# Gates of dense blocks scattered into cleared DRAM matrices by GpSimd, instead of built by one-hot products on TensorE

## The chip, the cores and the metric

The kernel runs on one core of a Trainium2 chip. The metric is the device time of one execution in microseconds; the kernel before took 3555.77 us (median of 3 runs, 3546.34 to 3557.35).

## What is computed

The reference is one decoder layer over 1024 tokens of width 1024: two mixers (sliding-window attention and a chunked mLSTM) make `x`, and then a PEER layer (an expert layer with 16384 experts of one hidden unit each) is added. The change touches the PEER layer alone:

```python
q = (xb @ w_query).reshape(t, PEER_HEADS, 2, PEER_KEY_DIM // 2)
s = jnp.einsum('thpd,hpkd->thpk', q, sub_keys)
top_s, top_i = lax.top_k(s, K)                     # K = 16 of 128, for both halves
cand_s = (top_s[:, :, 0, :, None] + top_s[:, :, 1, None, :]).reshape(t, PEER_HEADS, K * K)
cand_i = (top_i[:, :, 0, :, None] * N_KEYS + top_i[:, :, 1, None, :]).reshape(t, PEER_HEADS, K * K)
best_s, best_pos = lax.top_k(cand_s, K)
idx = jnp.take_along_axis(cand_i, best_pos, axis=-1)
gate = jax.nn.softmax(best_s, axis=-1)
act = jax.nn.gelu(jnp.einsum('td,thkd->thk', xb, expert_down[idx]), approximate=False)
out = jnp.einsum('thk,thkd->td', gate * act, expert_up[idx])
```

Each token picks 16 experts in each of 8 heads, 128 in all; two heads of a token may pick the same expert, and then their gates add up.

## The kernel before

The 1024 tokens are 8 blocks of 128, one token per partition, worked on in four groups of two blocks, (0,1) to (6,7). `front` runs the mixers of a group on TensorE: it ends with the output projection, whose four additions into `x` are L614 (called the x2 adds here), the PEER query and the scores, which go to DRAM (`sc_d`). `topk` then finds the experts of a block on VectorE. It is emitted by `later` with a low priority, so that the scheduler puts the top-k of one group between the rows of the next group's front. The weight strips of a front are split into a high and a low part, the low part on VectorE (L215, 50 such splits to a group), and TensorE waits for both.

PEER is worked out in two ways. Blocks 0, 6 and 7 (`SPARSE`) fetch the rows of their 128 experts by indirect DMAs from GpSimd (`fetch`, L743): per slot `down` gathers a row for every token and VectorE multiplies and sums it (L756), and `up` gathers another and VectorE adds it (L770). `down` of block 0 is run inside the fronts, its 128 sums spread over them by order edges (`pace`), with its gathers in a ring of two buffers. Blocks 1 to 5 (`DENSE`) go through all 16384 experts by matrix products (`dense`, in 32 steps of four rows of 128 experts): `hidden` makes the activations of all 640 tokens (L809), L816 multiplies them with a gate that is zero where a token did not pick the expert, and `outputs` adds the products with the up rows (L830 to L834).

That dense gate matrix is what the change is about. Before, `spread` makes it: the two parts of an expert's number and the gates are transposed, and for each token VectorE builds two one-hot matrices of 128x128 (L727 and L730; ScalarE makes one in four, L732 and L733), whose product over the token's 128 slots on TensorE (L735) is the token's 128x128 gate matrix; repeated experts add up in it. ScalarE copies four tokens to `stage` (L736), and 16 tokens go to `gate_d` by one DMA (L738), 64 numbers to a run. `fill` puts these quads between the rows of the last projections of the next group, three to every four pieces of a projection. A step of `dense` reads its 1280 KB of `gate_d` in one DMA (L841).

Each engine takes its instructions in the order in which the scheduler has put them into the program; the SP and GpSimd queues are in order too. DMAs from GpSimd signal through eight semaphores in turn (DMASW0 to 7), so the ninth waits for the first to land.

Of the kernel before, what the change touches and what calls it, by code (L numbers as in the profile page):

```python
# [10 lines left out]

F32 = mybir.dt.float32
# [5 lines left out]
AX = mybir.AxisListType  # L18
PSUM = bass.MemoryType.PSUM
NOSYNC = mybir.DependencyInfo(mybir.DependencyClass.NoSync, mybir.DependencyReason.DATA)  # L20

P = 128
S = 1024
# [11 lines left out]
SPARSE = (0, 6, 7)  # L35
DENSE = (1, 2, 3, 4, 5)
ND = P * len(DENSE)
GT = 16
GJ = 4
EG = 4  # L40
LATER = 5000
QUADS = 0.75
PACE0, PACE1 = 0.4, 0.95
WB = 4
PD0, PD1 = 0.06, 0.98
# [9 lines left out]
def layout(inputs):  # L55
# [5 lines left out]
    a = {}  # L61
# [21 lines left out]
    a["tri"] = tri  # L83
    a["freq"] = (500000.0 ** (-np.arange(0, 16, 2) / 16.0)).astype(np.float32)[None]
    a["iota"] = np.arange(P, dtype=np.float32)[None]
    return {k: np.ascontiguousarray(v) for k, v in a.items()}


def build(nc, tc, a, out, dbg=None):
# [4 lines left out]
    bp = pool("blocks", 2, outer)  # L94
    dp = pool("dram", 1, outer, space=bass.MemoryType.DRAM)
    kp = pool("topk", 2)
    ks = pool("spread", 1)
    gp = pool("gather", 2)
    st = pool("state", 1)
    wp = pool("weights", 1)  # L100
    fp = pool("front", 1)
# [8 lines left out]
    def const(name, shape, src=None, dt=F32, pool=None):  # L110
        t = (pool or cp).tile(shape, dt, name=name)
        SY.dma_start(t, a[name] if src is None else src)
        return t

    def probe(name, ap, idx=None):
        if dbg is not None and name in dbg:
            SY.dma_start(dbg[name] if idx is None else dbg[name][idx], ap)

    def bcast(name, n, pool=None):
        return const(name, [P, n], a[name].to_broadcast([P, n]), pool=pool)  # L120
# [10 lines left out]
    gains = const("gains", [P, 3, NC], pool=st)  # L131
    x_first = []
    pos = const("pos", [P, NB], dt=I32, pool=st)
    freq = bcast("freq", 8, st)
    qkg = bcast("qkg", 128, st)
    wifr = t4([P, NC, 16], "wifr")
# [54 lines left out]
    xb_d = dp.tile([NB, P, D], F32, name="xb_d")  # L191
    xbT_d = dp.tile([len(DENSE), P, NC, P], F32, name="xbT_d")
    sc_d = dp.tile([NB, 2, P, 8, P], F32, name="sc_d")
    gate_d = dp.tile([P, P // GJ, ND // GT, GJ, GT], F32, name="gate_d")

    RING = 3
    kT = st.tile([P, 2, RING, P], F32, name="kT")
# [9 lines left out]
    def wpart(i, q, split):  # L207
        t = wp.tile([P, 4, 256], F32, name="w", bufs=WB)
        SY.dma_start(t, a["wmain"][i, :, 4 * q:4 * q + 4, :])
        if not split:  # L210
            return t, None
        hi = wp.tile([P, 4, 256], F32R, name="whi", bufs=3)
        lo = wp.tile([P, 4, 256], F32R, name="wlo", bufs=3)
        A.copy(hi, t)  # L214
        V.tensor_tensor(lo, t, hi.bitcast(F32), ALU.subtract)  # L215
        return hi, lo
# [430 lines left out]
    def topk(b):  # L647
# [15 lines left out]
        for qh in range(4):  # L663
# [23 lines left out]
            for p, n in ((0, 17), (1, 16)):  # L687
# [4 lines left out]
                V.tensor_tensor(eqh, eqh, tif[:, :, p, None, 0:n].to_broadcast([P, 2, 16, n]), ALU.mult)  # L692
                V.tensor_reduce(ef[:, p, cols], eq, AX.X, ALU.add)
        gate = (bp.tile([P, 8, 16], F32, name="gate", bufs=len(SPARSE)) if b in SPARSE
                else ks.tile([P, 8, 16], F32, name="dgate", bufs=2))
        V.tensor_tensor(gate, bv, bv[:, :, 0:1].to_broadcast([P, 8, 16]), ALU.subtract)
        A.activation(gate, gate, AF.Exp)
        gs = kp.tile([P, 8], F32, name="gsum")
# [1 line left out]
        V.reciprocal(gs, gs)  # L700
        V.tensor_tensor(gate, gate, gs[:, :, None].to_broadcast([P, 8, 16]), ALU.mult)
        r = {"gate": gate}
        if b in SPARSE or dbg:
            r["idx"] = idx = bp.tile([P, P], I32, name="idx", bufs=len(SPARSE))
            V.scalar_tensor_tensor(idx, ef[:, 1], 128.0, ef[:, 0], ALU.mult, ALU.add)
            probe("idx", idx, b)
            probe("gate", gate, b)
        if b in DENSE:
            r["spread"] = spread(ef, gate, DENSE.index(b))
        return r  # L710

    def spread(ef, gate, k):
        cols = ks.tile([P, 3, P], F32, name="cols")
        ps = ptp.tile([P, 4, P], F32, name="tp")
        for n, src in enumerate((ef[:, 0], ef[:, 1], gate.rearrange("p h k -> p (h k)"))):
            T.transpose(ps[:, n, :], src, ident)
        A.copy(cols, ps[:, 0:3, :])
        for c in range(P // GT):
            stage = ks.tile([P, P, GT], F32, name="stage", bufs=2)
            for q in range(GT // 4):  # L720
                ps = pat.tile([P, 4, P], F32, name="at")
                for u in range(2):
                    oi = ks.tile([P, 2, P], F32, name="oi", bufs=3)
                    oj = ks.tile([P, 2, P], F32, name="oj", bufs=3)
                    t = c * GT + 4 * q + 2 * u
                    for n in range(2):
                        V.tensor_scalar(oi[:, n], iota, cols[:, 0, t + n:t + n + 1], cols[:, 2, t + n:t + n + 1],  # L727
                                        ALU.is_equal, ALU.mult)
                        if n or u:
                            V.tensor_scalar(oj[:, n], iota, cols[:, 1, t + n:t + n + 1], None, ALU.is_equal)  # L730
                        else:
                            A.activation(oj[:, n], iota, AF.Square, scale=-1.0, bias=cols[:, 1, t + n:t + n + 1])  # L732
                            A.activation(oj[:, n], oj[:, n], AF.Relu, scale=-1.0, bias=1.0)  # L733
                    for n in range(2):
                        T.matmul(ps[:, 2 * u + n, :], oi[:, n], oj[:, n], start=True, stop=True)  # L735
                A.copy(stage[:, :, 4 * q:4 * q + 4], ps.rearrange("p t j -> p j t"))  # L736
                if q == GT // 4 - 1:
                    SY.dma_start(gate_d[:, :, k * (P // GT) + c], stage.rearrange("p (n g) t -> p n g t", g=GJ))  # L738
                yield

    def fetch(p, table, idx, s):
        t = p.tile([P, D], F32, name="g")
# [31 lines left out]
    def dense():  # L774
# [26 lines left out]
        def hidden(j, g):  # L801
# [10 lines left out]
                    mark("dense", ins)  # L812
            act = tp.tile([P, ND], F32, name="act", bufs=1)
            A.activation(act.rearrange("p (u t) -> p u t", u=NH), ps[:, :, 0:W], AF.Gelu)
            av_ = act.rearrange("p (c t) -> p c t", t=GT)
            V.tensor_tensor(av_, av_, g, ALU.mult)  # L816
            ah = tp.tile([P, ND], F32R, name="ah", bufs=EG + 1)
            al = tp.tile([P, ND], F32R, name="al", bufs=EG + 1)
            A.copy(ah, act)
# [17 lines left out]

        work = []
        for n in range(P // EG):
            g = tp.tile([P, ND // GT, GJ, GT], F32, name="g")  # L840
            SY.dma_start(g, gate_d[:, n])  # L841
            new = []
            for e in range(EG):
                new.append(hidden(EG * n + e, g[:, :, e, :]))
                if n == 0 and e == 0:
                    for k in range(nk):
                        SY.dma_start(y[:, k, :], x2_d[DENSE[k]])
                if e == 0 and work:
                    outputs(work, new[0][3].ins.name)
            work = new  # L850
# [5 lines left out]
    def later(blocks):  # L856
        now = tc.cur_priority
        tc.cur_priority = now + LATER
        for b in blocks:
            res[b] = topk(b)  # L860
        tc.cur_priority = now
        return [q for b in blocks if "spread" in res[b] for q in [res[b]["spread"]]]

    res = {}
    hT = normed(GROUPS[0])
    for n, g in enumerate(GROUPS):
        spreads = chain.from_iterable(later(GROUPS[n - 1])) if n else iter(())

        due = [0.0]

        def fill():
            due[0] += QUADS
            while due[0] >= 1.0:
                next(spreads, None)
                due[0] -= 1.0

        hT = front(g, fill, hT, GROUPS[n + 1] if n + 1 < len(GROUPS) else None)
        for _ in spreads:
            pass
    later(GROUPS[-1])  # L880
    names = anchors["front"]
    names = names[int(PACE0 * len(names)):int(PACE1 * len(names))]
# [24 lines left out]
```

## Time and profile before

| | |
|---|---|
| median of 3 runs | 3555.77 us |
| the profiled execution | 3545.12 us, its span 3543.4 us |
| TensorE (PE) | 3378.6 us busy, 95% of the span |
| VectorE (DVE) | 2743.1 us, 77% |
| ScalarE (ACT) | 1363.0 us, 38% |
| GpSimd (POOL) | 985.7 us, 28% |
| TensorE's mean granted clock | 0.966 of full speed |

The profile is of one execution on the chip. Busy time is the time in which an engine runs an instruction; what an engine waited for is inferred from semaphores. The fronts of the four groups take the first half of the span, to about 1748 us, and the dense stage the rest.

### The profile page before, as it was taken

Reading aid. Unit: us, or ns where it says so; the run is one execution under the profiler, and the core shown is the slowest. Engines: PE = TensorE matmul, PEld = TensorE weight load, DVE = VectorE, ACT = ScalarE, POOL = GpSimd, SP = SyncE. Lnnn points to the kernel's source line nnn. Section 1 sums busy time; section 2 is a strip of 40 time slices with the busy share of each in tenths; the row PEclk is TensorE's granted clock in tenths of the full one; section 3 lists DMA queues with packets and bytes.
Section 4 is the critical chain, followed back from the end, with each engine's and each line's share of the span. In section 5 each row is a group of like instructions: output and inputs, shape, how many; then the busy total and the mean of one; then the engine's idle time right before and its main releaser. Section 6 shows DMA issues by size and latency. Waiting matters only on the chain.

```text
span 3543.4 us, 55473 instructions
## 1 busy us (share of the span) xinstructions
PE 3378.6 (95%) x20579; PEld 3044.3 (86%) x20579; DVE 2743.1 (77%) x6406; ACT 1363.0 (38%) x2730; POOL 985.7 (28%) x772
## 2 busy tenths in 40 slices
PE   7999999999998789989799999999999999999999
PEld 7898988888887678887688898999989999898998
DVE  5332689739898468988598988888888888889985
ACT  6652567338574346635322222222222222222221
POOL 0000000110001221110004654545455455545542
PEclk9999999999999888999899999999999999999999
DMA  4344434874378874686727988889888888888884
GB/s 149 108 143 166 164 115 145 256 261 141 117 212 252 274 247 150 206 244 174 252 101 276 329 307 321 321 284 329 285 315 305 294 321 299 312 308 302 325 288 160
DMA packets 386670, 846.66 MB, mean 239 GB/s; under 512 B 189280, under 2 KB 195168, under 8 KB 382304
## 3 DMA queue, kind: packets, MB, share of 16 engines
q1 hardware_dynamic: 275808, 440.42, 37.7%
q0 software_dynamic: 110592, 402.70, 32.5%
q8 instruction: 162, 2.65, 0.3%
q14 instruction: 108, 0.88, 0.1%
HBM read 780.11 MB, written 62.91 MB: 238 GB/s over the span
## 4 chain that ended last, share of the span: by engine, by line
PE 66%; DVE 13%; issue 8%; DMA 7%; POOL 3%; ACT 3%; SPq 0%; POOLq 0%; DVEq 0%; ACTq 0%
PE ph L809 19%; PE pj L229 8%; PE po L830 6%; PE po L833 6%; PE po L834 6%; PE pj L231 4%; PE pj L233 4%; PE pj L232 4%; DMA g<-down,idx 3%; POOL g L743 3%; DVE oi L727 2%; PE at L735 2%; DMA w<-wmain 1%; DVE g L756 1%; DMA g<-up,idx 1%
## 5 line engine op out<-in xcount | busy, mean ns | idle before, releaser
L743 POOL DMA_INDIRECT g<-down,idx x384 | 480.2, 1250 | 1769.3 <-DVE act L756 879.2
L743 POOL DMA_INDIRECT g<-up,idx x384 | 505.3, 1316 | 732.8 <-DVE acc L770 373.9
L756 DVE CUSTOM_DVE_ANT_0 g<-g,xb 128x1024 f32<-128x1024 f32 x384 | 462.6, 1219 | 167.2 <-DMA g<-down,idx 166.6
L770 DVE SCALAR_TENSOR_TENSOR acc<-g,coef,acc 128x1024 f32<-128x1024 f32 x384 | 491.7, 1281 | 46.8 <-DMA g<-up,idx 36.8
L830 PE MATMUL po<-hu,ah 128*128 128x512 f32 x1280 | 499.2, 390 | 2.3 <-DVE y L836 2.3
L809 PE MATMUL ph<-xbh,hd 128*128 128x320 f32 x2048 | 470.6, 311 | 31.7 <-ACT hd L797 22.8
L833 PE MATMUL po<-lu,ah 128*128 128x512 f32 x1280 | 498.5, 389 | 0.0
L834 PE MATMUL po<-hu,al 128*128 128x512 f32 x1280 | 498.1, 389 | 0.0
L809 PE MATMUL ph<-xbh,ld 128*128 128x320 f32 x2048 | 470.5, 311 | 5.3 <-DVE ld L798 5.3
L809 PE MATMUL ph<-xbl,hd 128*128 128x320 f32 x2048 | 469.9, 311 | 0.0
L797 ACT CAST hu<-rawu 128x1024 fp32r<-128x1024 f32 x128 | 131.5, 1051 | 738.9 <-PE po L834 557.0
L809 PEld LDWEIGHTS ph<-xbh,hd 128*128 128x128 f32 x2048 | 346.6, 189 | 35.3 <-ACT hd L797 23.2
L215 DVE TENSOR_TENSOR wlo<-w,whi 128x1024 fp32r<-128x1024 f32 x200 | 243.3, 1218 | 142.1 <-ACT whi L214 142.0
L809 PEld LDWEIGHTS ph<-xbh,ld 128*128 128x128 f32 x2048 | 345.1, 189 | 7.0 <-DVE ld L798 6.7
L809 PEld LDWEIGHTS ph<-xbl,hd 128*128 128x128 f32 x2048 | 345.6, 189 | 0.0
L214 ACT CAST whi<-w 128x1024 fp32r<-128x1024 f32 x200 | 209.3, 1047 | 235.9 <-DMA w<-wmain 100.1
L836 DVE TENSOR_TENSOR y<-po,y 128x512 f32<-128x512 f32 x320 | 218.2, 685 | 89.0 <-PE po L834 88.5
L830 PEld LDWEIGHTS po<-hu,ah 128*128 128x128 f32 x1280 | 240.3, 188 | 53.9 <-DVE y L836 4.7
L834 PEld LDWEIGHTS po<-hu,al 128*128 128x128 f32 x1280 | 240.3, 188 | 50.5 <-DVE al L820 0.3
L833 PEld LDWEIGHTS po<-lu,ah 128*128 128x128 f32 x1280 | 240.3, 188 | 48.5
L232 PE MATMUL pj<-wlo,hT 128*128 128x256 f32 x832 | 244.9, 295 | 23.9 <-DVE wlo L215 23.9
L231 PE MATMUL pj<-whi,hT 128*128 128x256 f32 x832 | 245.9, 296 | 1.1 <-ACT whi L214 1.1
(266 smaller groups left out, 6670.2 us busy)
## 6 DMA issues: line engine op xcount, KB each, us to landing
w<-wmain SPq DMA_DIRECT2D x328, 512.0 KB
rawd<-downT SPq DMA_DIRECT2D x128, 512.0 KB
rawu<-up SPq DMA_DIRECT2D x128, 512.0 KB
gate_d<-stage SPq DMA_DIRECT2D x40, 1024.0 KB
g<-gate_d SPq DMA_DIRECT2D x32, 1280.0 KB
x<-x SPq DMA_DIRECT2D x16, 512.0 KB
sc_d<-sc SPq DMA_DIRECT2D x16, 512.0 KB
sc<-sc_d SPq DMA_DIRECT2D x32, 256.0 KB
```

Source lines behind the costliest of these rows:

```text
L215: V.tensor_tensor(lo, t, hi.bitcast(F32), ALU.subtract)
L229: ins = T.matmul(ps, lh(c), rh(c), start=first, stop=last)
L231: T.matmul(ps, lh(c), rh(c), start=first, stop=False)
L232: T.matmul(ps, lh(c), rl(c), start=False, stop=False)
L743: G.indirect_dma_start(out=t, out_offset=None, in_=a[table], in_offset=bass.IndirectOffsetOnAxis(ap=idx[:, s:s + 1], axis=0))
L756: ins = V.tensor_tensor_reduce(out=t, in0=t, in1=xb, scale=1.0, scalar=0.0, op0=ALU.mult, op1=ALU.add, accum_out=act[:, s:s + 1])
L770: ins = V.scalar_tensor_tensor(acc, t, g, acc, ALU.mult, ALU.add)
L809: ins = T.matmul(ps[:, u, 0:W], w[:, c, :], x[:, c, u * W:u * W + W], start=first, stop=last)
L830: first = T.matmul(o, ah[:, tok], uh[:, cols], start=(e == 0), stop=False)
L833: T.matmul(o, ah[:, tok], ul[:, cols], start=False, stop=False)
L834: ins = T.matmul(o, al[:, tok], uh[:, cols], start=False, stop=(e == EG - 1))
L836: V.tensor_tensor(y[:, k, cols], o, y[:, k, cols], ALU.add)
```

## The change

`spread`, `fill` and `QUADS` go. For each dense block there is now a matrix `gate_d[k]` in DRAM, indexed by expert row, expert column and token (128x128x128, 8 MB). `clear_part` writes zeros to all five in 160 DMAs of 256 KB from SP, one behind each of the first 160 weight DMAs. `topk` of a dense block also makes `cell`, the address of each of its gates, and `scatter` then issues 128 indirect DMAs from GpSimd (L734 of the changed kernel), each of which adds the gates of one slot, 128 numbers of 4 bytes, into `gate_d[k]`. Within a head the experts of a token differ, so its 16 DMAs may run together; the first DMA of a head has to wait for all 16 of the head before, since two heads may add to the same cell. A step of `dense` reads its gates by five DMAs of 256 KB instead of one of 1280 KB, in runs of 512 bytes. The ring of `down`'s gathers in the fronts has four buffers instead of two.

```diff
+    tokc = const("tokc", [P, 1], pool=st)
@@
-    gate_d = dp.tile([P, P // GJ, ND // GT, GJ, GT], F32, name="gate_d")
+    gate_d = [dp.tile([P, P, P], F32, name=f"gate_d{b}") for b in DENSE]
+    none = st.tile([P, P * P // ZP], F32, name="none")
+    V.memset(none, 0.0)
+    clear = iter([(k, z) for k in range(len(DENSE)) for z in range(ZP)])
+
+    def clear_part():
+        for k, z in [next(clear, (None, 0))]:
+            if k is not None:
+                SY.dma_start(gate_d[k].rearrange("j i t -> (j i t)").rearrange("(z p f) -> z p f", z=ZP, p=P)[z], none)
@@ def wpart
         SY.dma_start(t, a["wmain"][i, :, 4 * q:4 * q + 4, :])
+        clear_part()
@@ def topk
         if b in DENSE:
-            r["spread"] = spread(ef, gate, DENSE.index(b))
+            cell = ks.tile([P, P], I32, name="cell")
+            V.tensor_scalar(cell, idx, 128.0, tokc, ALU.mult, ALU.add)
+            r["cell"] = cell
@@
-    def spread(ef, gate, k):
...
+    def scatter(rs):
+        views = [bass_types.dram_disjoint_views(gate_d[k].rearrange("j i t -> (j i t)")[:, None], 16) for k, _ in rs]
+        done = [[] for _ in rs]
+        for h in range(8):
+            for n, (k, r) in enumerate(rs):
+                new = []
+                for s in range(16):
+                    c = 16 * h + s
+                    ins = G.indirect_dma_start(
+                        out=views[n][s], out_offset=bass.IndirectOffsetOnAxis(ap=r["cell"][:, c:c + 1], axis=0),
+                        in_=r["gate"].rearrange("p h k -> p (h k)")[:, c:c + 1], in_offset=None, compute_op=ALU.add)
+                    if s == 0:
+                        for d in done[n]:
+                            tc.add_manual_dep(ins.ins, d, SYNC, reason="heads")
+                    else:
+                        after(ins, new[0])
+                    new.append(ins.ins.name)
+                done[n] = new
@@ def dense
-            g = tp.tile([P, ND // GT, GJ, GT], F32, name="g")
-            SY.dma_start(g, gate_d[:, n])
+            g = tp.tile([P, nk, EG, P], F32, name="g")
+            for k in range(nk):
+                SY.dma_start(g[:, k], gate_d[k][EG * n:EG * n + EG].rearrange("j i t -> i j t"))
@@
-    gp = pool("gather", 2)
+    gp = pool("gather", 4)
@@ def later
+        rs = [(DENSE.index(b), res[b]) for b in blocks if b in DENSE]
+        if rs:
+            scatter(rs)
```

How it moves the work shows in the order of the program. **GpSimd, from block 1's scatter on.** L747 is `fetch` (L743 before) and L734 a scatter; x32 stands for 32 equal rows. Before, GpSimd's order is 128 gathers of `down` and then those of the dense stage, with nothing between them:

```order
L743 DMA g<-down,idx 128x1024 x128
L743 DMA g<-up,idx 128x1024 x128
```

Now, from its first gather:

```order
L747 DMA g_15166<-down,idx_3600 128x1024
L734 DMA gate_d1_154<-dgate_3828,cell_3837 2097152x1 x32
L747 DMA g_15169<-down,idx_3600 128x1024
L747 DMA g_15172<-down,idx_3600 128x1024
L734 DMA gate_d1_154<-dgate_3828,cell_3837 2097152x1 x16
L747 DMA g_15175<-down,idx_3600 128x1024
L747 DMA g_15178<-down,idx_3600 128x1024
L734 DMA gate_d1_154<-dgate_3828,cell_3837 2097152x1 x16
```

The fourth gather of `down` is followed by 32 scatters, the sixth by 16 and so on; the 17th and 18th come behind all 128 scatters of block 1. Counted on in the same way, gathers 39 to 77 have 161 scatters of blocks 2 and 3 among them, gathers 78 to 93 the other 95, gathers 114 to 128 have 96 scatters of block 4, and none stands between 94 and 113.

**VectorE, at the x2 adds of group 1** (L625 there, L614 before; L760 is the sum over a gathered row, L756 before). The rows now, with the 15th to 18th sum of `down`:

```order
L760 ISA g_15199,act_15151<-g_15199,xb_15152 128x1024
L760 ISA act_15151 128x1
L625 TENSOR_TENSOR x_6822<-pj_6826,x_6822 128x512
L760 ISA g_15202,act_15151<-g_15202,xb_15152 128x1024
L760 ISA act_15151 128x1
L625 TENSOR_TENSOR x_6824<-pj_6827,x_6824 128x512
L760 ISA g_15205,act_15151<-g_15205,xb_15152 128x1024
L760 ISA act_15151 128x1
L760 ISA g_15208,act_15151<-g_15208,xb_15152 128x1024
L760 ISA act_15151 128x1
L625 TENSOR_TENSOR x_6822<-pj_6874,x_6822 128x512
L625 TENSOR_TENSOR x_6824<-pj_6875,x_6824 128x512
```

The order of the x2 adds and sums here is the one before too: the last two adds stand behind sum 18. In group 2 they stand behind sum 77 (before, behind sum 59). The cells of block 2 are made behind sum 34, those of block 4 behind sum 109 and those of block 5 behind sum 126, ahead of the x2 adds of group 3; sum 93 stands ahead of the 18th weight split of group 3.

**GpSimd and SP, at the start of the dense stage.** The end of GpSimd's fronts, from its last gather of `down`:

```order
L747 DMA g_15538<-down,idx_3600 128x1024
L734 DMA gate_d4_157<-dgate_11177,cell_11186 2097152x1 x16
L734 DMA gate_d5_158<-dgate_11414,cell_11423 2097152x1 x16
...
L734 DMA gate_d4_157<-dgate_11177,cell_11186 2097152x1 x4
L734 DMA gate_d5_158<-dgate_11414,cell_11423 2097152x1 x64
L747 DMA g_28977<-up,idx_3600 128x1024
```

and SP's first loads for the dense stage, with what they wait for:

```order
L845 DMA g<-gate_d_156 128x4x128 [waits DMAHW0_49]
L845 DMA g<-gate_d_157 128x4x128 [waits DMASW4_49,DMASW5_49,DMASW3_49,DMASW6_49,DMASW2_49,DMASW7_49,DMASW1_49,DMASW0_49]
L845 DMA g<-gate_d_158 128x4x128 [waits DMASW5_49,DMASW4_49,DMASW6_49,DMASW3_49,DMASW7_49,DMASW2_49,DMAHW2_49,DMASW1_49,DMASW0_49]
L798 DMA rawd<-downT 128x1024 [waits DMAHW3_49,DVE_49]
L798 DMA rawu<-up 128x1024 [waits DMAHW4_49,DVE_49]
```

160 scatters stand between the last gather of `down` and the first of `up`: the last 32 of block 4, and all 128 of block 5. The gate loads wait for all eight semaphores of GpSimd's DMAs, and the first expert tables of the dense stage (`rawd`, `rawu`) are behind them on SP.

## Rows read from the trace of the kernel before

**Rows 1.** Page, part 1; instruction groups (busy us, mean ns | idle before us).

```profile
PE 3378.6 (95%) x20579; PEld 3044.3 (86%) x20579; DVE 2743.1 (77%) x6406; ACT 1363.0 (38%) x2730; POOL 985.7 (28%) x772
...
L727 DVE TENSOR_SCALAR oi<-iota,cols 128x128 f32<-128x128 f32 x640 | 203.3, 342 | 9.8 <-PE at L735 6.8 <-ACT cols L717 2.9
L735 PE MATMUL at<-oj,oi 128*128 128x128 f32 x1280 | 201.6, 290 | 23.1 <-DVE oj L730 13.1 <-DVE oi L727 5.0 <-ACT oj L733 4.8
...
L730 DVE TENSOR_SCALAR oj<-iota,cols 128x128 f32<-128x128 f32 x480 | 133.7, 280 | 0.0
```

**Rows 2.** Windows, fronts and dense: PE, PEld, DVE, ACT, POOL busy; clock; DMA share.

```profile
0.00:1748.00 1748.00, 1603.23 (x10643) 1424.42 (x10643) 1214.02 (x4306) 921.43 (x2190) 142.59 (x132) 0.94 0.60 188
1748.00:3543.40 1795.40, 1775.36 (x9936) 1619.91 (x9936) 1529.06 (x2101) 441.58 (x542) 843.09 (x640) 1.00 0.81 288
```

**Rows 3.** Windows of groups 1 to 3, L735 alone: PE, PEld busy; clock; DMA share.

```profile
374.00:781.00 407.00, 39.76 (x256) 35.38 (x256) 0.95 0.58 184
781.00:1247.00 466.00, 79.38 (x512) 72.71 (x512) 0.93 0.66 204
1247.00:1714.00 467.00, 82.44 (x512) 73.02 (x512) 0.93 0.66 202
```

**Rows 4.** Waits, 781 to 1714 us: us in total, times, longest.

```profile
DVE g L756 <- DMA g<-down,idx: 95.4, 38, 5.8
```

**Rows 5.** GpSimd, 560 to 1610 us: its group; its instructions, min/median/max ns.

```profile
L743 POOL DMA_INDIRECT g<-down,idx x126 | 140.4, 1114 | 947.4 <-DVE act L756 610.9 <-DVE rs_t L167 119.1 <-DVE oi L727 106.4
...
L743 POOL DMA_INDIRECT g<-down,idx x126: 937/940/1912, 647.8 to 1589.8; - x126
```

**Rows 6.** Timeline of GpSimd: start, us, instruction, idle before in brackets.

```profile
1883.14 0.94 POOL L743 DMA_INDIRECT g<-up,idx  x1 [0.30 <-issue]
1884.39 0.94 POOL L743 DMA_INDIRECT g<-up,idx  x1 [0.30 <-issue]
```

**Rows 7.** Chain, landing of a gather; timeline, a small load and its user.

```profile
651.21 8.77 DMA g<-down,idx
...
2.60 0.43 SPq L112 DMA_DIRECT2D pos<-pos  x1
...
4.94 0.17 DVE L174 CAST tmp<-pos 128x8 f32<-128x8 int32 x1 [3.55 <-DMA pos<-pos]
```

**Rows 8.** Timeline of VectorE: gates, x2 adds, a weight split, the first gating.

```profile
587.55 0.28 DVE L701 TENSOR_TENSOR dgate<-dgate,gsum 128x128 f32<-128x128 f32 x1
...
732.00 0.69 DVE L614 TENSOR_TENSOR x<-pj,x 128x512 f32<-128x512 f32 x1 [1.04 <-PE pj L229]
...
897.30 0.28 DVE L701 TENSOR_TENSOR dgate<-dgate,gsum 128x128 f32<-128x128 f32 x1
...
1179.41 0.68 DVE L614 TENSOR_TENSOR x<-pj,x 128x512 f32<-128x512 f32 x1
...
1325.56 1.18 DVE L215 TENSOR_TENSOR wlo<-w,whi 128x1024 fp32r<-128x1024 f32 x1
...
1453.91 0.28 DVE L701 TENSOR_TENSOR dgate<-dgate,gsum 128x128 f32<-128x128 f32 x1
...
1748.05 0.82 DVE L816 TENSOR_TENSOR act<-act,g 128x640 f32<-128x640 f32 x1
```

**Rows 9.** Timeline of SP's queue at the start of the dense stage.

```profile
1726.14 0.43 SPq L841 DMA_DIRECT2D g<-gate_d  x1
1727.63 0.33 SPq L794 DMA_DIRECT2D rawd<-downT  x1
```

**Rows 10.** Page, parts 2 and 3: packets; queues with packets, MB, share.

```profile
DMA packets 386670, 846.66 MB, mean 239 GB/s; under 512 B 189280, under 2 KB 195168, under 8 KB 382304
...
q1 hardware_dynamic: 275808, 440.42, 37.7%
q0 software_dynamic: 110592, 402.70, 32.5%
```

More of the change, by code (lines that the diff above doesn't have):

```diff
@@ L8 @@
 import concourse.tile as tile
+from concourse import bass_types
 from concourse import mybir
@@ L20 @@
 NOSYNC = mybir.DependencyInfo(mybir.DependencyClass.NoSync, mybir.DependencyReason.DATA)
+SYNC = mybir.DependencyInfo(mybir.DependencyClass.Sync, mybir.DependencyReason.DATA)
 P = 128
@@ L37 @@
 ND = P * len(DENSE)
-GT = 16
-GJ = 4
 EG = 4
+ZP = 32
 LATER = 5000
-QUADS = 0.75
 PACE0, PACE1 = 0.4, 0.95
@@ L85, in layout @@
     a["iota"] = np.arange(P, dtype=np.float32)[None]
+    a["tokc"] = np.arange(P, dtype=np.float32)[:, None]
     return {k: np.ascontiguousarray(v) for k, v in a.items()}
@@ L96, in build @@
     kp = pool("topk", 2)
-    ks = pool("spread", 1)
-    gp = pool("gather", 2)
+    ks = pool("scatter", 2)
+    gp = pool("gather", 4)
     st = pool("state", 1)
@@ L694, in topk @@
         gate = (bp.tile([P, 8, 16], F32, name="gate", bufs=len(SPARSE)) if b in SPARSE
-                else ks.tile([P, 8, 16], F32, name="dgate", bufs=2))
+                else ks.tile([P, 8, 16], F32, name="dgate"))
         V.tensor_tensor(gate, bv, bv[:, :, 0:1].to_broadcast([P, 8, 16]), ALU.subtract)
@@ L702, in topk @@
         r = {"gate": gate}
[L703 to L707, printed above, removed]
+        r["idx"] = idx = (bp.tile([P, P], I32, name="idx", bufs=len(SPARSE)) if b in SPARSE
+                          else ks.tile([P, P], I32, name="didx"))
+        V.scalar_tensor_tensor(idx, ef[:, 1], 128.0, ef[:, 0], ALU.mult, ALU.add)
@@ L708, in topk @@
+        probe("idx", idx, b)
+        probe("gate", gate, b)
         if b in DENSE:
-            r["spread"] = spread(ef, gate, DENSE.index(b))
-        return r
-    def spread(ef, gate, k):
[L713 to L739, printed above, removed]
@@ L814, in hidden @@
             A.activation(act.rearrange("p (u t) -> p u t", u=NH), ps[:, :, 0:W], AF.Gelu)
-            av_ = act.rearrange("p (c t) -> p c t", t=GT)
-            V.tensor_tensor(av_, av_, g, ALU.mult)
+            V.tensor_tensor(act.rearrange("p (k t) -> p k t", t=P), act.rearrange("p (k t) -> p k t", t=P), g, ALU.mult)
             ah = tp.tile([P, ND], F32R, name="ah", bufs=EG + 1)
@@ L860, in later @@
             res[b] = topk(b)
+        rs = [(DENSE.index(b), res[b]) for b in blocks if b in DENSE]
+        if rs:
+            scatter(rs)
         tc.cur_priority = now
-        return [q for b in blocks if "spread" in res[b] for q in [res[b]["spread"]]]
     res = {}
@@ L866, in build @@
     for n, g in enumerate(GROUPS):
[L867 to L879, printed above, removed]
+        if n:
+            later(GROUPS[n - 1])
+        hT = front(g, nothing, hT, GROUPS[n + 1] if n + 1 < len(GROUPS) else None)
     later(GROUPS[-1])
```

## The prediction

> **What bounds the kernel now.** I read the page first, then the windows, then the order of the program against the timeline. TensorE is busy 95% of the span, VectorE 77%, GpSimd 28% [rows 1]. By stage this holds for TensorE in both halves: 1603 of 1748 us in the fronts, 1775 of 1795 in the dense stage, while GpSimd works 143 us in the fronts and 843 in the dense stage [rows 2]. So in the fronts GpSimd has room, and TensorE has none. Of TensorE's time there 202 us are the products L735 of one-hot matrices [rows 1], 40, 79 and 82 us of them in groups 1, 2 and 3 [rows 3]; VectorE spends 203 + 134 = 337 us on making the matrices [rows 1]. In groups 2 and 3 VectorE also waits 95 us for `down`'s gathers [rows 4]. One execution is worked with: 3545.12 us, span 3543.4; the median of the runs is 10.7 us above it, 0.3%, which is also about what a measurement of this kernel can tell from no change.
>
> **What is removed.** Up to 202 us of TensorE, all on the path as long as TensorE sets the pace of the fronts, and part of the 95 us of gather waits, by the deeper ring. Alone this would bring the first gating of the dense stage (L816) from 1748 [rows 8] to 1546 or somewhat below. The stage writes also leave the DMA queues. At the rate of GpSimd's queue, 402.70 MB in 32.5% of the span, or 2.86 us per MB, SP's other 398.5 MB would take 32.2%, so the 41.9 MB of stage writes take the other 5.5%, 195 us, some 19 ns for each of 163840 packets [rows 10].
>
> **What is added on the queues.** The clears are as many MB in longer runs, at 2.86 us per MB 120 us of the engines: less than leaves, in fronts where DMA is busy 0.60 of the time [rows 2]. Their 160 issues at some 0.43 us on SP [rows 7] are spread over two fronts; I cost them at nothing, at most 10 us of late weights. The dense reads become 81920 packets of 512 bytes, at most 2 x 19 ns each, 195 us against 120 us at the old rate: 75 us more over 1795 us raises the DMA share there from 0.81 [rows 2] to 0.85. TensorE still covers it; 0 to 75 us, and I take 0.
>
> **What is added on GpSimd.** 640 scatters. A gather of 128 rows takes 1114 ns on average in the fronts, from 937 to 1912 with a median of 940 [rows 5], and 0.30 us pass between two in a row [rows 6]. A scatter has as many addresses, so I look for the same price, and not for less because it moves 512 bytes: 1.24 us is the low end (0.94 + 0.30), 2.21 the high end (1.91 + 0.30). I take 1.5, near the mean of the gathers (1.41) with something for the additions. The trace has no adding DMA. What the first scatter of a head waits for the 16 before lies between the small load's 2.3 us from issue to its user and the gather's 8.8 us [rows 7], less the issue itself: 1 to 7 us; I take 3, and 2 where a gather or the other block's head stands in between. The Trainium skill (DMA: Bandwidth & Descriptors, section "Anatomy of one DMA") gives about 2.0 us of fixed time to each such DMA, most of it the receipt of the write; with 2 in place of 3 the sum below would be some 10 us lower, and no row here shows a receipt by itself.
>
> 640 x 1.5 = 960 us would fit into the 1160 from 588 to 1748 us if they lay evenly. It doesn't, since GpSimd's order is fixed and `down`'s gathers, on which VectorE waits, stand between the scatters. I follow the places where VectorE must wait for GpSimd; times of before are those of [rows 8], a gather lands and is summed in 9 us [rows 7].
> 1. Block 1's cells are ready at 588, as before. The last x2 add of group 1 stands behind sum 18, whose gather is behind 128 scatters and 14 gathers: 142 x 1.5 = 213, one uncovered wait 3, landing 9: 813. Before it was 732.
> 2. From there to the cells of block 2 nothing of L735 leaves and no scatter stands in the way: 897 - 732 = 165, so 978.
> 3. The last x2 add of group 2 is behind sum 77: 161 scatters and 39 gathers, 200 x 1.5 = 300, ten head waits of 2, landing 9: 1307. TensorE's own way is 1179 - 897 = 282, less 79 of L735: 203, shorter. Before: 1179.
> 4. To block 4's cells 1454 - 1179 = 275 us pass, again without L735. In them sum 93 stands ahead of a weight split that came 146 us behind the x2 add, and its gather is behind 95 scatters and 16 gathers, 167 us and some 10 of waits, begun 9 us before the sum's landing was used: 30 us late. So 1307 + 275 + 30 = 1612.
> 5. Behind them 96 scatters of block 4 and 15 gathers: 111 x 1.5 + 6 x 2 = 179, to 1791. Block 5's cells come in this stretch.
> 6. Then the 160 scatters that stand behind the last gather: 240, and 9 for the last heads, which are block 5's alone: 2040. SP's gate loads wait for the last of them, 3 us, and the first tables of the experts are behind these on SP. From the gate load to the first gating it took 1748 - 1726 = 22 us before [rows 8, 9]: 2065.
>
> 2065 - 1748 = 317 us later. From there the dense stage runs as before, bound by TensorE, with the same 640 gathers: 3545 + 317 = 3862, rounded to **3860 us**. What TensorE and VectorE no longer do becomes waiting, for gathers in groups 1 to 3 and for the tail at the end. On the path lie 613 issues (142, 200, 111 and 160), and 30 us of the fourth step. At 1.24 us each with short waits it is 159 + 30 + some 20 less, 3650; at 2.21 with long waits 435 + 79 + some 60 more, near 4430.
>
> **Rivals.**
> - *GpSimd keeps up, and it gets faster.* If a scatter cost 0.7 us, the chain would be 613 x 0.8 = 490 and the 30 us shorter: 1545, just TensorE's own 1546, and the time 3545 - 202 = 3343, some tens less with the gather waits gone. The point from which it decides is where the chain gives 1748: 287 / 613 = 0.47 less, about 1.0 us per scatter. For it: 512 bytes instead of 512 KB. Against it: the time on GpSimd is that of issuing, not of moving, and of 126 gathers none took less than 0.94 [rows 5]. Chance 0.09.
> - *The landing binds.* GpSimd has eight DMAs under way. If an adding write of single numbers lands in over 8 x 1.5 = 12 us, each scatter waits for the eighth before it. At 20 us a scatter costs 2.5: 613 more, 111 in the fourth step, some 100 for head waits: 4690. For it: 8.8 us of a gather among weight loads, and a read has to come before each write. Against it: the small load's 2.3 us. Chance 0.12 for anything over 4350. The Trainium skill (same page, "Rules for kernel authors") says that transfers under 64 KB are mostly overhead and should be joined, which speaks against 640 DMAs of 512 bytes; were 2.0 us paid for each in turn, the sum would be 613 x 0.5 + 56 more, 4224, which the gathers' 1.24 us in a row do not bear out.
> - *A draw.* Scatters near 1.0 us: within 11 us of 3545 or of the median. Chance 0.03.
>
> **How the numbers follow.** The forecast, GpSimd's chain with 1.24 to 2.1 us per scatter, has 0.76, and the time is its middle, 3860. The range runs from its low end, 3640, to 4350: it leaves out the faster rival and the draw below, and the binding landing above. The cases below 3545 have 0.09, no change 0.03, slower 0.88.
>
> **What would show it.** GpSimd busy 700 us or more longer, in nearly unbroken rows from about 590 to 2040 us; a scatter at 0.9 to 1.6 us with 0.3 between; VectorE waiting for `down`'s gathers by hundreds of us in place of 95; TensorE's gaps in groups 1 to 3 and a still TensorE for some 70 us or more before the dense stage, with the gate loads held by DMASW; first gating near 2065; from there to the end 1795 us. It is wrong if scatters show under 1.0 us, if the first gating is before 1748, or if the dense stage is what grows.

## The result, and the profile after

The changed kernel takes **4145.0 us** (median of 4 runs, 4143.72 to 4156.52), against 3555.0 for the kernel before (4 runs): a ratio of 1.167, 95% interval 1.164 to 1.170. Slower was forecast, and the time lies in the range of 3640 to 4350, but 285 us above the 3860 that was named. The profiled execution has a span of 4144.0 us.

The page of the changed kernel: part 1, and two of the costliest groups of part 5 (busy us, mean ns | idle time before, and what ended it).

```profile
PE 3269.8 (79%) x19284; PEld 2933.7 (71%) x19284; DVE 2488.4 (60%) x5297; ACT 1185.2 (29%) x2250; POOL 2026.8 (49%) x1412
...
L734 POOL DMA_INDIRECT gate_d<-dgate,cell x640 | 1037.5, 1621 | 338.8 <-issue 198.9
...
L760 DVE CUSTOM_DVE_ANT_0 g<-g,xb 128x1024 f32<-128x1024 f32 x384 | 462.5, 1219 | 747.5 <-DMA g<-down,idx 747.1
```

TensorE falls from 95% [rows 1] to 79%: it has less to do and waits more. GpSimd gains 1041 us, and the scatters are 1037.5. The last line is where the time shows: VectorE stands 747 us for `down`'s gathers. In the kernel before, its row has 167, of which 95 are in groups 2 and 3 [rows 4]:

```profile
L756 DVE CUSTOM_DVE_ANT_0 g<-g,xb 128x1024 f32<-128x1024 f32 x384 | 462.6, 1219 | 167.2 <-DMA g<-down,idx 166.6
```

The windows, cut where the prediction's steps end (PE, PEld, DVE, ACT and POOL busy with instructions; TensorE's granted clock; DMA share; GB/s):

```profile
594.00:868.00 274.00, 109.92 (x565) 97.17 (x564) 46.06 (x88) 23.45 (x43) 225.64 (x146) 0.70 0.47 88
868.00:1063.00 195.00, 184.29 (x1255) 157.36 (x1256) 134.93 (x470) 113.46 (x279) 19.44 (x17) 0.89 0.54 183
1063.00:1452.00 389.00, 201.97 (x1077) 176.80 (x1076) 149.85 (x471) 71.89 (x153) 313.27 (x203) 0.73 0.55 122
1452.00:1805.00 353.00, 231.65 (x1554) 205.24 (x1555) 165.54 (x528) 134.33 (x311) 192.26 (x129) 0.76 0.52 138
1805.00:2021.00 216.00, 123.87 (x626) 107.51 (x626) 96.60 (x359) 42.09 (x95) 173.47 (x112) 0.74 0.51 107
2021.00:2344.00 323.00, 81.26 (x406) 70.65 (x404) 38.32 (x143) 29.79 (x60) 250.13 (x161) 0.62 0.42 72
```

The first, third, fifth and sixth rows are the bursts: GpSimd is busy 77 to 82% there, and the gaps between its issues fill the rest, while TensorE works 25 to 57% of the time. The second row is the stretch without scatters: TensorE busy 184 of 195 us. The dense stage is as before: 1777.16 us of TensorE in the 1800 from 2344 to the end, against 1775 in 1795 [rows 2].

The timeline of GpSimd inside the burst for blocks 2 and 3 (start, us, instruction, idle time before it):

```profile
1200.13 1.54 POOL L734 DMA_INDIRECT gate_d<-dgate,cell  x1 [0.30 <-issue]
1201.98 1.54 POOL L734 DMA_INDIRECT gate_d<-dgate,cell  x1 [0.30 <-issue]
```

One scatter every 1.85 us, where two gathers stood 1.24 us apart [rows 6]. For all 640, the view of the line (min/median/max in ns; then idle time and number):

```profile
L734 POOL DMA_INDIRECT gate_d<-dgate,cell x640: 1541/1542/2689, 594.0 to 2324.7; - x160
...
  issue: 198.9, 606
  DVE cell L721: 105.5, 2
  DMA gate_d<-dgate,cell: 32.9, 27
```

Half of the scatters take 1.54 us to within a nanosecond; the longer ones bring the mean to 1.62 (1621 ns on the page). Of waiting for earlier scatters there are only 32.9 us in all.

The timeline of VectorE at the ends of the steps: the cells of blocks 1, 2 and 4, and the last x2 adds of groups 1 (the second of the two in its row) and 2.

```profile
593.39 0.29 DVE L721 TENSOR_SCALAR cell<-didx,tokc 128x128 int32<-128x128 int32 x1
...
867.01 1.28 DVE L625 TENSOR_TENSOR x<-pj,x 128x512 f32<-128x512 f32 x2
...
1062.56 0.27 DVE L721 TENSOR_SCALAR cell<-didx,tokc 128x128 int32<-128x128 int32 x1
...
1451.56 0.69 DVE L625 TENSOR_TENSOR x<-pj,x 128x512 f32<-128x512 f32 x1
...
1804.69 0.28 DVE L721 TENSOR_SCALAR cell<-didx,tokc 128x128 int32<-128x128 int32 x1
```

The tail, first on SP's queue, then in the waits (us in total, times, longest):

```profile
2327.88 0.36 SPq L845 DMA_DIRECT2D g<-gate_d  x1
2328.34 0.45 SPq L798 DMA_DIRECT2D rawd<-downT  x1
2328.89 0.37 SPq L798 DMA_DIRECT2D rawu<-up  x1
```

```profile
DVE g L760 <- DMA g<-down,idx: 747.1, 89, 41.4
PE ph L813 <- DMA rawu<-up: 233.2, 1, 233.2
```

The last scatter is issued at 2324.7, the gate load goes out 3 us later and the first tables of the experts behind it. TensorE, with nothing left of the fronts, stood still for 233 us in one piece. The first gating (L819) comes at 2344, where 2065 was forecast and 1748 was before [rows 8].

### The profile page after: what moved, and what is told of

Read it like the earlier page. It is cut to its first block, busy times and chain, and to the rows that moved or that the text cites. A ratio compares the mean times of both kernels' runs of the same rounds, so it can differ in the third digit from the quotient of the medians.

```text
span 4144.0 us, 52025 instructions
## 1 busy us (share of the span) xinstructions
PE 3269.8 (79%) x19284; PEld 2933.7 (71%) x19284; DVE 2488.4 (60%) x5297; ACT 1185.2 (29%) x2250; POOL 2026.8 (49%) x1412
## 4 chain that ended last, share of the span: by engine, by line
PE 29%; POOL 9%; issue 6%; DVE 4%; DMA 3%; ACT 0%; SPq 0%; POOLq 0%; DVEq 0%; ACTq 0%
PE ph L813 14%; POOL gate_d L734 6%; PE po L837 5%; PE po L833 5%; PE po L836 5%; POOL g L747 3%; DMA rawu<-up 1%; DMA g<-up,idx 1%; DVE acc L774 1%; DMA gate_d<-dgate,cell 0%; DMA g<-down,idx 0%; DVE ld L802 0%; DVE y L839 0%; DVE lu L802 0%; DVE act L819 0%
## 5 line engine op out<-in xcount | busy, mean ns | idle before, releaser
L734 POOL DMA_INDIRECT gate_d<-dgate,cell x640 | 1037.5, 1621 | 338.8 <-issue 198.9
L747 POOL DMA_INDIRECT g<-down,idx x384 | 481.4, 1254 | 1128.2 <-DVE sc L668 501.2
L760 DVE CUSTOM_DVE_ANT_0 g<-g,xb 128x1024 f32<-128x1024 f32 x384 | 462.5, 1219 | 747.5 <-DMA g<-down,idx 747.1
L747 POOL DMA_INDIRECT g<-up,idx x384 | 507.6, 1322 | 594.8 <-DVE acc L774 378.1
L774 DVE SCALAR_TENSOR_TENSOR acc<-g,coef,acc 128x1024 f32<-128x1024 f32 x384 | 491.4, 1280 | 42.9 <-DMA g<-up,idx 33.4
L802 DVE TENSOR_TENSOR ld<-rawd,hd 128x1024 fp32r<-128x1024 f32 x128 | 156.1, 1219 | 216.9 <-ACT hd L801 216.8
L242 PE MATMUL pj<-hT,whi 128*128 128x256 f32 x768 | 237.6, 310 | 58.7 <-DVE gs L613 36.0
```

The costliest lines, as they stand in the source:

```text
L242: T.matmul(ps, lh(c), rh(c), start=first, stop=False)
L734: ins = G.indirect_dma_start(out=views[n][s], out_offset=bass.IndirectOffsetOnAxis(ap=r["cell"][:, c:c + 1], axis=0), in_=r["gate"].rearra ...
L747: G.indirect_dma_start(out=t, out_offset=None, in_=a[table], in_offset=bass.IndirectOffsetOnAxis(ap=idx[:, s:s + 1], axis=0))
L760: ins = V.tensor_tensor_reduce(out=t, in0=t, in1=xb, scale=1.0, scalar=0.0, op0=ALU.mult, op1=ALU.add, accum_out=act[:, s:s + 1])
L774: ins = V.scalar_tensor_tensor(acc, t, g, acc, ALU.mult, ALU.add)
```

## The experiments

My theory: GpSimd's issue of each scatter is the cost, and `down`'s gathers and the gate loads queue behind it. The rivals: the scatters' landing, their transfers, or the rest of the change (clears, cells, loads by block). All but the last two are single executions. They ran on chips on which the kernel before took 3549 to 3562 us, so differences of some 10 us between them say nothing.

**The addition taken away.** Plain writes in place of adding ones; gates of a cell that two heads share are then not summed.

```diff
-    in_=r["gate"].rearrange("p h k -> p (h k)")[:, c:c + 1], in_offset=None, compute_op=ALU.add)
+    in_=r["gate"].rearrange("p h k -> p (h k)")[:, c:c + 1], in_offset=None)
```

> Leaves out the adding: the scatters are plain writes in the same order and with the same waits between heads, so where two heads of a token pick the same expert one gate is lost. Theory (the price of issuing an adding scatter on GpSimd, 1.97 us apart in the mean, 1.54 us of it on the engine): without the addition a scatter takes what a gather takes, 0.94 to 1.1 us and 0.3 between; 613 issues on the path become 0.6 to 0.7 us shorter, 370 to 430 us in all, so 3720 to 3780 us. Rival (the landing and the head waits set the pace): the scatters come no closer than before, waits take the place of the shorter issue, and the time stays above 4050 us.

Measured: 3786.9 us, just above the band of 3720 to 3780. The group of the scatters on the page, then the view of the line with its landing times, which count from the start of the issue:

```profile
L734 POOL DMA_INDIRECT gate_d<-dgate,cell x640 | 661.5, 1034 | 350.9 <-issue 204.8
```

```profile
L734 POOL DMA_INDIRECT gate_d<-dgate,cell x640: 952/958/2596, 598.6 to 1965.5; - x160
...
DMA to landing us min/median/max: 2.1/2.8/7.3
```

An issue costs 0.96 us, as a gather of 128 rows did [rows 5]; the addition is worth 1.54 - 0.96 = 0.58. Over the 640 scatters GpSimd saves 1037.5 - 661.5 = 376 us, and the kernel gives back 4145.0 - 3786.9 = 358: nearly all of the scatters' issue time lies on the path. Even a plain scatter, at 0.96 + 0.30, leaves the kernel slower than before.

**Fewer scatters.** Two of the eight heads are scattered (the gates of the other six are left out).

```diff
-        for h in range(8):
+        for h in range(2):
```

> Leaves out the gates of heads 2 to 7 of the dense blocks: 32 scatters to a block instead of 128, all else (clears, dense reads, gather ring, order rules) as in the change. Theory (GpSimd's order is what the time is made of): with 160 scatters in place of 640 the chain leaves the path, TensorE sets the pace of the fronts again, and the time is that of before less the 202 us of one-hot products and some of the gather waits: 3270 to 3370 us. Rival (clears, 512-byte reads of the gates, or the new order itself cost the time): 3545 us or more.

Measured: 3428.5 us, some 60 above the expected band. The issue stayed at 1.54 us. A burst of 32 still stands ahead of gathers that VectorE needs: in the fronts it waits 146 us for `down` (25 times, up to 41.6), more than the 125 of the kernel before. The scatters' whole price falls with their number, but that of a burst ahead of a gather does not vanish.

**The gathers moved out of the way.** Block 0's 128 gathers and sums go to the dense stage, so that no gather of the fronts stands behind a scatter.

```diff
...
-    down(res[0], 0, pace, gp)
     inner.close()
     gd = dense()
...
+    down(res[0], 0, pace, gd)
```

> Moves all 128 gathers and sums of block 0 from the fronts into the dense stage, so that nothing in the fronts waits for GpSimd; the 640 scatters stay. Theory (VectorE's sums in a fixed order carry GpSimd's delay into the fronts): the fronts run at TensorE's pace, and the scatters, 1.9 us each, end some 500 us behind the cells of block 4 or of the blocks before, at 1800 to 1900 us; first gating near 1880 instead of 2344, and the dense stage, with 166 us more on a VectorE that is 85 percent busy, takes 1800 to 1900 us: 3670 to 3800 us in all. Rival (the scatters themselves are late whatever is between them): first gating after 2200, 4000 us or more.

Measured: 3882.2 us, above the band. The windows from group 1's front to the end, and one wait of VectorE after 1059:

```profile
374.00:694.00 320.00, 316.98 (x2174) 283.28 (x2174) 215.06 (x814) 168.84 (x394) 77.24 (x48) 0.95 0.50 143
694.00:1059.00 365.00, 354.13 (x2332) 312.41 (x2330) 218.05 (x822) 181.12 (x428) 282.23 (x169) 0.95 0.63 144
1059.00:1525.00 466.00, 355.49 (x2326) 315.68 (x2326) 209.88 (x796) 168.86 (x402) 360.73 (x222) 0.84 0.53 110
1525.00:1944.00 419.00, 47.80 (x256) 42.18 (x256) 33.30 (x132) 27.94 (x59) 316.81 (x203) 0.56 0.32 42
1944.00:3880.00 1936.00, 1820.55 (x9936) 1637.48 (x9936) 1675.93 (x2359) 442.67 (x542) 1060.21 (x768) 0.98 0.87 303
```

```profile
DVE dgate L707 <- DMA gate_d<-dgate,cell: 103.4, 1, 103.4
```

In its first two rows TensorE is free (317 of 320 and 354 of 365 us), with GpSimd scattering beside it: it was the queue that held the fronts, not the transfers. What I had not counted: the gates and cells have two buffers, and a later block's topk waits 103 us for one that scatters still read. The 640 scatters themselves then end at 1924, some 400 us behind the fronts' last x2 add, and the dense stage, which now has the 128 gathers and sums, grows to 1936. Queue and total are two costs, and this removes only the first.

**More waits.** Every eighth scatter waits for the eight before it, 40 waits more.

```diff
-                    if s == 0:
-                        for d in done[n]:
+                    if s % 8 == 0:
+                        for d in (new if s else done[n]):
```

> Doubles the waits: the scatters of a head wait for all before them after eight as well as after sixteen, 40 waits more. Theory (issue price): a wait costs the 1 to 3 us by which the landing of the last one exceeds the next issue, and some are covered by gathers between: 30 to 120 us more, 4175 to 4270 us. Rival (the landing sets the pace): each of the 40 waits costs a landing of 7 us or more, 280 us and up, over 4400 us.

Measured: 4147.7 us, no more than single executions differ by, under the expected band. The view of the line, idle time for its own DMAs and landing:

```profile
  DMA gate_d<-dgate,cell: 36.0, 35
...
DMA to landing us min/median/max: 2.9/3.1/9.5
```

A scatter lands 3 us after the start of its issue, when the one behind it is all but issued. So waiting for it costs a fraction of a microsecond, whether there are 40 more waits or not: 36.0 us in place of 32.9. The rival of the landing falls.

**No scatter at all.** The dense blocks' gates are left out; cells, clears and loads stay.

```diff
         if rs:
-            scatter(rs)
+            pass
```

> The changed kernel without any of its 640 scatters (the dense blocks' gates are left out: their matrices stay zero); the cells, the clearing and the loads by block stay. This gives what the removal of the one-hot products is worth by itself, and so the size of the scatters' whole cost. If the queue behind the scatters is the one cause (my theory), groups 1 and 2 run at the pace that the kernel without block 0's gathers in the front showed (320 and 365 us, against 359 and 447 before), the first gating comes between 1480 and 1640, and the time is between 3290 and 3450 us. If the rest of the change (cells, clears by 160 DMAs, five loads for one) costs something too, the time is above 3560, though no scatter is left.

Measured: 3311.5 us, inside the band, with the line of the first gating at

```profile
L819 DVE TENSOR_TENSOR act<-act,g x128: 809/818/830, 1512.2 to 3278.7; 128x640 f32<-128x640 f32 x128
```

With no scatter to stand behind, the fronts end at 1512. The clears, cells and loads by block cost little, if anything: 3549 us before on this chip, less the 202 of one-hot products and some 50 that the longer ring is worth (below), would be 3297. The scatters' whole price is 4145.0 - 3311.5 = 833 us.

**Half of the addresses.** Each scatter takes 64 tokens (the gates of the other 64 are left out).

```diff
-    out=views[n][s], out_offset=bass.IndirectOffsetOnAxis(ap=r["cell"][:, c:c + 1], axis=0),
-    in_=r["gate"].rearrange("p h k -> p (h k)")[:, c:c + 1], in_offset=None, compute_op=ALU.add)
+    out=views[n][s], out_offset=bass.IndirectOffsetOnAxis(ap=r["cell"][0:64, c:c + 1], axis=0),
+    in_=r["gate"].rearrange("p h k -> p (h k)")[0:64, c:c + 1], in_offset=None, compute_op=ALU.add)
```

> Each of the 640 scatters takes 64 tokens in place of 128 (the gates of the other 64 tokens are left out), the number of instructions stays. If GpSimd's price is by address (addition included), an issue falls from 1.54 us to 0.75-0.95, the spacing from 1.85 to about 1.1-1.25, and 613 issues on the path give back 370-460 us: 3690-3780. If the price is by instruction, the issue stays at 1.5 us and the time at 4100-4150.

Measured: 4055.7 us, by neither; nearer to the price by instruction.

```profile
L734 POOL DMA_INDIRECT gate_d<-dgate,cell x640: 1392/1402/3520, 593.2 to 2232.6; - x160
```

Half of the addresses save 0.14 of 1.54 us; 640 x 0.14 = 90 us, and the kernel gives back 89. By these two points the other 1.26 us come with the instruction, so a scatter of few numbers is no cheaper way.

**Hybrids of the kernel before.** If a scatter is harmless where GpSimd has room, some blocks could be scattered two at a time between gathers and the others made by one-hot products. First blocks 1 and 2, then 1 to 3; the diff is to the kernel before, for the two-block kernel.

```diff
+SCAT = (1, 2)
+SPANS = ((0.36, 0.66), (0.66, 0.95))
...
-    gp = pool("gather", 2)
+    gp = pool("gather", 3)
...
-            stage = ks.tile([P, P, GT], F32, name="stage", bufs=2)
+            stage = ks.tile([P, P, GT], F32, name="stage", bufs=1)
...
-                    oi = ks.tile([P, 2, P], F32, name="oi", bufs=3)
-                    oj = ks.tile([P, 2, P], F32, name="oj", bufs=3)
+                    oi = ks.tile([P, 2, P], F32, name="oi", bufs=2)
+                    oj = ks.tile([P, 2, P], F32, name="oj", bufs=2)
...
+    for k, b in enumerate(SCAT):
+        f0, f1 = SPANS[k]
+        scatter(k, res[b], iter([names[int((f0 + i * (f1 - f0) / P) * len(names))] for i in range(P)]))
```

> The kernel before with the scatters for blocks 1 and 2 alone (256 of 640), two between one gather and the next in place of bursts of a block, the other three blocks by one-hot products (for space the gather ring is 3, the staging one buffer). By the queue theory a scatter is harmless where GpSimd has room: 256 x 1.85 = 474 us go into a front of 1370 us in which GpSimd is busy for 143, and a gather comes at most some 6 us late; what is left is the one-hot work saved of two blocks, some 40 us each: 3450-3500. If the adding scatters themselves (their transfers, GpSimd's port) slow the rest, 3560 or more.

> As the one with two blocks, with blocks 1, 2 and 3 (384 scatters, 2 to 3 between gathers; 384 x 1.85 = 710 us of GpSimd, with the 128 gathers some 870 of 1370). Queue theory: GpSimd still has room, three blocks' one-hot work is saved: 3400-3470. If GpSimd's load as such is what counts, it is above the two-block kernel.

Measured: 3493.6 us for two blocks, against 3549.2 before, as expected; 3594.3 for three, slower than before and far above the band. The gain of the first seemed to speak for the theory, but it had three pool sizes in it besides, so these were run alone, as a control without any scatter (the hunks on `gp`, `stage`, `oi` and `oj` above):

> The kernel before with only the buffers of the two- and three-block kernels (gather ring 3 in place of 2, staging one buffer in place of two, one-hot pairs two in place of three), no scatter. If the two-block kernel's gain of 56 us comes from the one-hot work that it saves, this one stays within 20 us of the kernel before (3530-3570). If it comes from the longer gather ring, this one is at 3490-3510 too.

Measured: 3498.4 us, against 3554.3. **The buffers alone give the two-block kernel's gain.** The longer ring is the part of the edit that answers to it in the waits. VectorE's wait for `down`'s gathers from 374 to 1750 us, in the kernel before, the control and the two-block kernel (its timed run):

```profile
DVE g L756 <- DMA g<-down,idx: 125.1, 49, 5.8
```

```profile
DVE g L756 <- DMA g<-down,idx: 29.4, 17, 4.8
```

```profile
DVE g L798 <- DMA g<-down,idx: 141.5, 41, 17.9
```

The ring of three takes 96 us off these waits; 256 scatters put 112 on again. By GpSimd's timeline mostly one to three of them stand between a gather and the next, as intended, but rows of 18, 18 and 30 are among them. And the windows of group 2's front, from x2 add to x2 add, of the control, then of the two-block kernel:

```profile
726.00:1163.00 437.00, 413.05 (x2808) 363.74 (x2808) 363.34 (x1326) 249.03 (x607) 49.28 (x45) 0.96 0.67 208
```

```profile
714.00:1153.00 439.00, 396.16 (x2589) 346.63 (x2589) 332.07 (x1152) 221.19 (x525) 244.28 (x162) 0.93 0.72 205
```

TensorE has 17 us less to do in this front, and the front takes 2 us more. So the saved one-hot work is given back as waiting, with GpSimd only 56% busy: room on average was not room at the time. That the issues do this, and not the scatters' transfers, was shown for the changed kernel above and not tested again here.

One try to better it: head 0 of a block written plainly, since nothing lies under it yet, and the scatters a little earlier.

```diff
-SPANS = ((0.36, 0.66), (0.66, 0.95))
+SPANS = ((0.36, 0.58), (0.58, 0.9))
...
-    in_offset=None, compute_op=ALU.add)
+    in_offset=None, compute_op=ALU.add if h else ALU.bypass)
```

> The two-block kernel, with head 0 of each block written plainly (nothing but cleared cells under it, so the sum is the same) and the scatters spread a little earlier. By the measured prices 32 of 256 issues cost 0.96 in place of 1.54 us: 19 us of GpSimd, and GpSimd is not the limit for most of the front, so 0 to 25 us less than the 3493.6 of the two-block kernel: 3470-3495. If a scatter's price to the front is its transfers and not GpSimd's time, nothing changes.

Measured: 3524.1 us, worse and outside of the band: VectorE's wait for the gathers rose to 157.7 us in the same stretch. Two edits went in together, so the runs do not tell which did it; denser scatters fit the longer wait, cheaper ones do not.

The two-block kernel timed:

> The two-block kernel again, unchanged, timed against the kernel before: 3485-3500, a ratio of 0.980 to 0.988.

Measured: 3504.0 us (3495.7 to 3517.4, 4 runs), a ratio of 0.987, interval 0.985 to 0.990. The median lies just above the band of 3485 to 3500.

And the control with a ring of four:

```diff
-    gp = pool("gather", 3)
+    gp = pool("gather", 4)
```

> The control with a gather ring of 4 in place of 3 (one-hot work for all five blocks as before, no scatter). The ring of 3 took 3498 and left 67 us of VectorE's waits for gathers in place of 167 over the whole kernel. If a gather that is issued earlier is what the front wants, the fourth buffer takes some of the rest: 3470-3498. If the ring of 3 was enough, it stays at 3490-3505. Either way it stays under the two-block kernel's 3504 and under the kernel before: a ratio of 0.975 to 0.988.

Measured: 3502.2 us (3496.7 to 3507.1, 5 runs) against 3549.1, a ratio of **0.986, interval 0.985 to 0.988**. The waits are 21.4 us in place of 29.4: three buffers were enough. This version, one-hot products and no scatter, is 1.4% faster than the kernel before, little but beyond its interval, and as fast as the two-block hybrid.

## Why the prediction was right in direction and short by 285 us

*What is removed* was sized well. Without scatters the first gating came at 1512, where "1546 or somewhat below" stood. Of the gain, some 50 us can be had without the change, by the buffers.

*The price of a scatter* is the term that was too small: "I take 1.5, near the mean of the gathers (1.41) with something for the additions". It was 1.54 for the issue and 0.30 after it, 1.85 in a row. The additions alone are 0.58, and what was put in for them was 0.09. The high end of 2.21 held it. At 1.85 the 613 issues give 613 x 0.35 = 215 us more. That 1.85 fits all 613 is in part luck: 68 of them are gathers, which cost less, and the 545 scatters cost more in the mean (1.62 for the issue) than at the median. In the first window the two together take 225.64 us for 146 issues, 1.55 each before the 0.30.

*The waits* were taken too long: 3 us for a head alone and 2 with something between; measured were 32.9 us over 27 waits in the whole kernel, 1.2 each. The landing, 3 us by the median of the run with more waits, is mostly spent inside the next issue.

*The steps*, each from the end of the one before (us):

| step | foretold | measured | what the difference holds |
|---|---|---|---|
| 1, block 1's cells to group 1's last x2 add | 225 | 274 | 142 x 0.35 = 50 |
| 2, to block 2's cells | 165 | 196 | no scatter in it; see below |
| 3, to group 2's last x2 add | 329 | 389 | 200 x 0.35 = 70, less for waits |
| 4, to block 4's cells | 305 | 353 | the late sum: 111 x 0.35 = 39; 5 as in step 2 |
| 5, to the last gather, 2021 | 179 | 216 | 111 x 0.35 = 39 |
| 6, to the first gating | 274 | 323 | 160 x 0.35 = 56, less for waits |

The differences are 49, 31, 60, 48, 37 and 49. With the 5 us by which block 1's cells came later they make up the 279 us between 2065 and 2344; the dense stage adds 5 (1800 against 1795). The queue's way through the kernel was right: VectorE waits 206, 228, 166 and 112 us for the gathers in steps 1, 3, 4 and 5, and 4 in step 2. Its price was not, nor was the moment at which the cells are ready.

*Step 2* had an assumption of its own: it took the gates of the kernel before (L701, at 897) for the moment at which the cells are ready. The cells need the block's last expert numbers as well, and these can come later. The second window, cut once more, and VectorE's timeline at the gates and behind them:

```profile
868.00:1036.00 168.00, 157.29 (x1159) 140.42 (x1160) 120.25 (x434) 107.00 (x260) 16.03 (x15) 0.95 0.58 196
1036.00:1063.00 27.00, 27.00 (x98) 16.93 (x98) 14.69 (x37) 6.46 (x19) 3.41 (x3) 0.57 0.31 107
```

```profile
1041.09 0.28 DVE L712 TENSOR_TENSOR dgate<-dgate,gsum 128x128 f32<-128x128 f32 x1
...
1049.69 1.29 DVE L516 TENSOR_TENSOR WT<-at,WT 128x512 f32<-128x512 f32 x2 [5.78 <-PE at L513]
...
1061.37 0.68 DVE L704 TENSOR_REDUCE ef<-eq 128x32 f32<-128x512 f32 x1
```

The first 168 us are the 165 of before (there 1152 matmuls in 155.65 us of TensorE, at a clock of 0.96), so the stretch without scatters did run nearly as foretold. The gates come at 1041, 8 us later than foretold from the x2 add, and the cells 21 us behind them. In between VectorE works on the mLSTM and waits for its products on TensorE, and only then makes the last expert numbers (L704). In the kernel before these numbers came ahead of that work:

```profile
904.04 0.67 DVE L693 TENSOR_REDUCE ef<-eq 128x32 f32<-128x512 f32 x1
...
910.00 1.29 DVE L505 TENSOR_TENSOR WT<-at,WT 128x512 f32<-128x512 f32 x2 [4.45 <-PE at L502]
```

TensorE is busy throughout the 27 us, at a granted clock of 0.57, so mostly at the lower of its two levels (1.2 GHz); in the 168 us ahead, 94% busy, it had 0.95. In steps 1 and 4 the cells came 3 and 5 us behind the gates. Some 30 us of the 285 are this, and not the price of a scatter.

Over the whole kernel the same 19284 matmuls took 3269.8 us of TensorE here and 3190.7 without scatters, 79 us that no term of the sum had. 78 of them lie ahead of the first gating, where TensorE also waits most; how much of them is on the path was not measured.

*The rivals.* "GpSimd keeps up" needed about 1.0 us per scatter; it got 1.85, and the plain scatter, at 1.26, also stayed on the slower side. Its best case of 3343 was a fair figure for no scatter (3311.5). "The landing binds" did not happen: 3.1 us is far from 12. The Trainium skill (DMA: Bandwidth & Descriptors, section "Anatomy of one DMA") gives about 2.0 us of fixed time to each such DMA. The plain scatter is near that: from the start of its issue it lands after 2.1 us at the shortest and 2.8 at the median. The sum of 4224 that came of paying 2.0 us in turn is near 4145 by chance: when 40 waits for landing were added, the time did not move beyond noise.

*No cost on the queues* was right: clears and cells show next to nothing in the kernel without scatters, and the dense stage's DMA share rose to 0.84, where 0.85 was foretold.

## What to carry to other kernels

Price an indirect DMA by its issue on GpSimd, and by every later instruction of that queue for which somebody waits; bytes and landing tell little, and an adding one is to be priced by itself. An engine's free share of a stage says nothing until the order of its queue is held against the moments at which others need it: 256 scatters in a half-empty GpSimd ate all that they saved. And run the side edits of a change (here the buffers) alone before its main part is credited.

## What was not expected of the hardware

An addition lengthens the issue of a 128-address scatter from 0.96 to 1.54 us. The software queue's packets, part 3 of the page, for no scatter, plain, half of the addresses adding, and all adding:

```profile
q0 software_dynamic: 110592, 402.70, 34.3%
```

```profile
q0 software_dynamic: 131072, 403.07, 30.6%
```

```profile
q0 software_dynamic: 161792, 402.91, 32.1%
```

```profile
q0 software_dynamic: 202752, 403.07, 33.9%
```

Over the 110592 of the gathers these are 32, 80 and 144 packets per scatter. These two counts of the adding scatter fit one packet per address and 16 more (64 + 16, 128 + 16), where the plain one gets by with 32 in all. But the issue time does not follow the packets: 64 addresses fewer save 0.14 us, and the step from 32 packets to 80 costs 0.44. What of the 1.26 us by instruction GpSimd spends on which part, no run here shows.
